# Forgetting attention's output projection: two weight splits earlier in the program, squares on ScalarE

## The chip, the cores and the metric

The kernel runs on one core of a Trainium2 chip. The metric is the device time of one execution in microseconds (us); the median of several runs counts. TensorE multiplies matrices, VectorE, ScalarE and GpSimd do elementwise work, SyncE (SP) issues most of the DMAs. In the profile's rows PE is TensorE and PEld its weight loads, DVE is VectorE, ACT is ScalarE, POOL is GpSimd; L105 is line 105 of the kernel.

## The reference

A two-layer transformer on 512 tokens of width 1024: layer 0 is forgetting attention (16 heads of 64) and a convolutional feed-forward layer, layer 1 is latent attention and another such feed-forward layer. What the change touches is the end of layer 0's attention and the beginning of its feed-forward layer:

```python
    o = lax.map(block, (jnp.arange(s_len // QBLOCK), to_blocks(q), to_blocks(cum)))
    return from_blocks(o).reshape(b, s_len, FOX_WIDTH) @ w_out
...
            x = x + fox_mixer(rmsnorm(x, fox_norm[layer]), w_fox_in[layer], b_fox_f[layer],
                              w_fox_out[layer])
...
        x = x + conv_ffn(rmsnorm(x, ffn_norm[layer]), w_ffn_in[layer], ffn_conv_w[layer],
                         ffn_conv_b[layer], w_ffn_out[layer])
```

All values are float32. So the output projection is a 512 x 1024 by 1024 x 1024 product, added to x; the root mean square of the new x over its 1024 features then scales the input of the feed-forward layer.

## The kernel before, in words

Activations lie transposed in SBUF, features on the partitions: `xT` has eight tiles of 128 features by 512 tokens. Each float32 operand of a product is split into a high part, rounded to the format that TensorE takes, and a low part, the rest; a product of a weight block with an activation block is three matmuls (`mm3`: high by high on L83, high by low on L84, low by high on L85). A step here is one such triple.

`load_w` brings in a weight. SP loads it into one of three `raw` buffers (L95), ScalarE casts it to the high part (L104), and the engine `eng`, VectorE if none is given, subtracts that from the raw weight (L105), which gives the low part. By default both go into the tags `whi` and `wlo`, of two buffers each.

The output projection has eight output tiles of 128 features, eight steps each. `wo_tile(d, pt, early)` makes a generator that does one step each time it is asked. Tiles 0 to 4 are begun inside the loop over the heads, one step at a time, to fill TensorE's holes (`FOX_FILL`); tiles 0 and 1 hold the two pairs of `whi` and `wlo`, while the weights of tiles 2 to 4 lie in buffers of the attention that are already free, loaded in halves. `fill((4,) * 7)` behind the loop does seven steps of tile 4. Each of the five has its eighth step left.

`out_proj` then takes the tiles in turn. For each it finishes the steps, adds the result in PSUM to `xT` on VectorE (L264), and splits the sum, times a gain, for the feed-forward layer: the high part on ScalarE (L188), the low part on VectorE (L189). The sum's square goes into the running sum of squares. For tiles 0 to 6 the square is a multiplication on GpSimd (L141), for tile 7 an activation on ScalarE (L139); GpSimd adds all of them up (L145). Squares and sum take buffers of the tag `r2`, of which there are four. The weights of tiles 5, 6 and 7 are loaded and split when their tile's turn comes in the program.

The feed-forward layer begins with weight blocks `in_wfi` and a step for each of the eight split tiles; the reciprocal root of the sum of squares is applied to its results, so that it is wanted only behind its first tile (L153).

Each engine executes its own instructions in order. Their order is the text's, as far as a scheduler of the framework, which lays the instructions of the whole program out before the run, doesn't let one go ahead whose operands it expects earlier.

Of the kernel before, what the change touches and what calls it, by code (L numbers as in the profile page):

```python
# [15 lines left out]
P = 128  # L16
# [3 lines left out]
KD = D // P  # L20
# [14 lines left out]
G_FOX, G_FFN, G_KVIN, G_MLA, G_KV, G_Q, G_FIN, G_N = 0, 8, 24, 32, 40, 42, 48, 56  # L35
# [10 lines left out]
def tile_kernel(ctx, tc, xT_d, gains_d, bf_d, const_d, conv_d, wv_d, wq_d, wk_d, wfo_d,  # L46
                wdq_d, wdkv_d, wuqn_d, wuqr_d, wuk_d, wuv_d, wmo_d, wfi_d, wfu_d, out_d):
    nc = tc.nc
    v, a, g, pe = nc.vector, nc.scalar, nc.gpsimd, nc.tensor
# [11 lines left out]
    def T(pool, shape, dt, tag, bufs=None):  # L61
        cnt[0] += 1
        kw = {} if bufs is None else {"bufs": bufs}
        return pool.tile(shape, dt, tag=tag, name=f"{tag}_{cnt[0]}", **kw)

    def acc():
        return T(ps, [P, 512], F32, "acc", 3)

    def att():
        return T(ps, [P, 512], F32, "att", 5)  # L70
# [4 lines left out]
    def big(k, name):  # L75
        return T(bp, [P, 8, 2, S], F32R, "big", 3)[:, :k]

    def f(ap):
        return ap.bitcast(F32)
# [7 lines left out]
    def load_w(src, shape, gain=None, eng=None, into=None, pieces=1):  # L87

        n = 1
        for s in shape[1:]:  # L90
            n *= s
        raw = T(wp, [P, 1024], F32, "raw", 3)[:, :n]
        cuts = [slice(i * n // pieces, (i + 1) * n // pieces) for i in range(pieces)]
        for c in cuts:
            nc.sync.dma_start(raw[:, c], src[:, c])  # L95
        if gain is not None:
            k, c = gain
            r3 = raw.rearrange("p (k c) -> p k c", c=n // k)
            g.tensor_tensor(out=r3, in0=r3, in1=c.unsqueeze(2).to_broadcast([P, k, n // k]), op=ALU.mult)
        if into is None:  # L100
            into = T(wp, [P, 1024], F32R, "whi", 2), T(wp, [P, 1024], F32R, "wlo", 2)
        hi, lo = (t[:, :n] for t in into)
        for c in cuts:
            a.copy(hi[:, c], raw[:, c])  # L104
            (eng or v).tensor_tensor(out=lo[:, c], in0=raw[:, c], in1=f(hi[:, c]), op=ALU.subtract)  # L105
        names = " ".join(f"d{i}" for i in range(len(shape) - 1))
        kw = {f"d{i}": shape[i + 1] for i in range(len(shape) - 1)}
        pat = f"p ({names}) -> p {names}"
        return hi.rearrange(pat, **kw), lo.rearrange(pat, **kw)
# [5 lines left out]
    def gain(base, k):  # L115
        return gains[:, base + k:base + k + 1]

    xT = cp.tile([P, KD, S], F32, name="xT")
# [63 lines left out]
    def split_x(dst, k, src, gn):  # L182

        if gn is None:
            a.copy(dst[:, k, 0, :], src)  # L185
            v.tensor_tensor(out=dst[:, k, 1, :], in0=src, in1=f(dst[:, k, 0, :]), op=ALU.subtract)
        else:
            a.activation(dst[:, k, 0, :], src, AF.Copy, scale=gn)  # L188
            v.scalar_tensor_tensor(out=dst[:, k, 1, :], in0=src, scalar=gn, in1=f(dst[:, k, 0, :]),  # L189
                                   op0=ALU.mult, op1=ALU.subtract)  # L190

    def parts(t, k, sl=slice(None)):
        return t[:, k, 0, sl], t[:, k, 1, sl]
# [52 lines left out]
    def out_tile(pt, loads, nk, src):  # L246

        k = 0
        for load, kn in loads:
            wh, wl = load()  # L250
            for kk in range(kn):
                mm3(pt, (wh[:, kk, :], wl[:, kk, :]), src(k), k == 0, k == nk - 1)
                k += 1
                yield

    def out_proj(tile_of, gbase):

        xs = big(KD, "xs")
        squares = Squares()
        for d in range(KD):  # L260
            pt, steps = tile_of(d)
            for _ in steps:
                pass
            v.tensor_tensor(out=xT[:, d, :], in0=pt, in1=xT[:, d, :], op=ALU.add)  # L264
            split_x(xs, d, xT[:, d, :], None if gbase is None else gain(gbase, d))
            squares.add(xT[:, d, :], a if d == KD - 1 else g)
        return xs, squares

    class Rstd:
# [19 lines left out]
    def ffn(layer, xs, squares, gbase):  # L289
        with tc.tile_pool(name=f"ffn{layer}", bufs=1, reuse_waits="tile") as fp:  # L290
# [42 lines left out]
            if layer < DEPTH - 1:  # L333
                return out_proj(tile_of, gbase)
# [66 lines left out]
    with tc.tile_pool(name="fx", bufs=1, reuse_waits="tile") as fp:  # L401
# [5 lines left out]
        squares = Squares()  # L407
# [107 lines left out]
        def proj_q(j):  # L515
            wh, wl = load_w(wq_d[j], [P, KD, P], eng=g)
            pt = acc()
            for k in range(KD):
                mm3(pt, (wh[:, k, :], wl[:, k, :]), parts(xn, k), k == 0, k == KD - 1)
                if k < KD - 1:  # L520
                    yield
            for e in range(2):
                t1 = T(fp, [P, S], F32R, "t1", 4)
                t2 = T(fp, [P, S], F32R, "t2", 4)
                nc.gpsimd.dma_start(t2[64:68], cum_d[0, 2 * j + e])
                src = pt[64 * e:64 * e + 64, :]
                a.activation(t1[0:64], src, AF.Copy, scale=FSCALE)
                v.scalar_tensor_tensor(out=t1[64:128], in0=src, scalar=FSCALE, in1=f(t1[0:64]),
                                       op0=ALU.mult, op1=ALU.subtract)
                a.copy(t2[0:64], f(t1[0:64]))  # L530
                qs[2 * j + e] = t1, t2
            yield

        def proj_k(j):
            wh, wl = load_w(wk_d[j], [P, KD, P], eng=g)
            pt = acc()
            for k in range(KD):
                mm3(pt, (wh[:, k, :], wl[:, k, :]), parts(xn, k), k == 0, k == KD - 1)
                if k < KD - 1:
                    yield  # L540
            for e in range(2):
                m1 = T(fp, [P, S], F32R, "m1", 2)
                m2 = T(fp, [P, S], F32R, "m2", 2)
                nc.gpsimd.dma_start(m2[64:68], cum_d[1, 2 * j + e])
                src = pt[64 * e:64 * e + 64, :]
                a.copy(m1[0:64], src)
                v.tensor_tensor(out=m2[0:64], in0=src, in1=f(m1[0:64]), op=ALU.subtract)
                a.copy(m1[64:128], f(m1[0:64]))
                ks[2 * j + e] = m1, m2
            yield  # L550

        def scores(h):
            (t1, t2), (m1, m2) = qs.pop(h), ks.pop(h)

            def passes(i, n):
                sl = slice(i * P, (i + 1) * P)
                return [(t1[:, sl], m1[:, :n]), (t2[0:68, sl], m2[0:68, :n])]

            es_h, softmax = attn_scores(fp, lambda: by_tile(passes), mask)
            softmax()  # L560
            return es_h
# [11 lines left out]
        def wo_tile(d, pt, early):  # L573
            def load(c):
                tags = (("m1", 2), ("m2", 2)) if d == 4 else (("t1", 4), ("t2", 4))
                into = [T(fp, [P, S], F32R, t, n) for t, n in tags]
                return load_w(wfo_d[d, :, c * S:(c + 1) * S], [P, KD // 2, P], eng=g, into=into)

            loads = [(lambda c=c: load(c), KD // 2) for c in (0, 1)] if early else [(lambda: load_w(wfo_d[d], [P, KD, P]), KD)]
            return pt, out_tile(pt, loads, KD, lambda k: parts(oT, k))  # L580

        def fillers():
            for j in range(1, FH // 2):
                yield from proj_q(j)
                yield from proj_k(j)
# [2 lines left out]
            for _ in u:  # L588
                pass
        es = {0: scores(0)}  # L590
        stream, ahead = fillers(), {}

        def fill(what):
            if isinstance(what, int):
                for _ in range(what):
                    next(stream)
            else:
                for d in what:
                    if d not in ahead:
                        ahead[d] = wo_tile(d, acc() if d < 2 else att(), d >= 2)  # L600
                    next(ahead[d][1])

        fill(12)
        for h in range(FH):
# [7 lines left out]
            values(h, pT, op_t)  # L612
            if h % 2:
                split_x(oT, h // 2, op_t, None)
        fill((4,) * 7)

        xs, squares = out_proj(lambda d: ahead[d] if d in ahead else wo_tile(d, acc(), False), G_FFN)

    xs, squares = ffn(0, xs, squares, None)


    with tc.tile_pool(name="ml", bufs=1, reuse_waits="tile") as mp:
# [107 lines left out]
        squares = Squares()  # L730
# [21 lines left out]
        squares = Squares()  # L752
# [16 lines left out]
        def mo_tile(d, pt):  # L769
            return pt, out_tile(pt, [(lambda c=c: load_w(wmo_d[d, :, c * D:(c + 1) * D], [P, 8, P]), 8) for c in (0, 1)],  # L770
                                MH, lambda k: parts(oTs[k // 8], k % 8))

        ahead = {}
# [16 lines left out]
        for h in range(MH):  # L790
# [23 lines left out]
            mvalues(h, pT)  # L814

        xs, squares = out_proj(lambda d: ahead[d] if d in ahead else mo_tile(d, acc()), G_FFN + KD)

    ffn(1, xs, squares, None)
# [88 lines left out]
```

## Time and profile before

| | |
|---|---|
| median of 3 runs | 1411.13 us |
| lowest and highest run | 1409.04 and 1411.53 us |
| the profiled execution, its own time | 1410.6 us |
| its span, first to last instruction | 1408.8 us |
| mean granted clock of TensorE | 0.993 |
| busy: TensorE, VectorE, ScalarE, GpSimd | 1373.6, 886.6, 648.7, 282.2 us |

The profile comes from one execution; times inside it count from the span's start. The stage of the change lies between about 234 and 270 us. The granted clock is 1.00 at 2.4 GHz and 0.50 at 1.2 GHz.

### The profile page before, as it was taken

What the parts mean: (1) busy time and instruction counts of PE and PEld (TensorE: products, weight loads), DVE (VectorE), ACT (ScalarE), POOL (GpSimd) and SP (SyncE); (2) the same over time, 40 slices, a digit from 0 to 9 for tenths busy, and PEclk for the clock granted to TensorE, in tenths of its full rate; (3) what the DMA queues carried; (4) which work ended last, traced back from release to release, by engine and by line L of the source; (5) the groups of instructions that cost most, each with busy time, mean ns of one, the idle gap of its engine ahead of it and who ended that gap; (6) DMA issues with size and microseconds to landing.
All of it is one profiled execution on the core that took longest, in us unless ns stands there. A gap on an engine that the chain in (4) does not pass through costs nothing. (4 is left out here: it accounts for less than half of the span.)

```text
span 1408.8 us, 17333 instructions
## 1 busy us (share of the span) xinstructions
PE 1373.6 (98%) x6594; PEld 1150.8 (82%) x6594; DVE 886.6 (63%) x1482; ACT 648.7 (46%) x1131; POOL 282.2 (20%) x214
## 2 busy tenths in 40 slices
PE   8999999899999999999899999999999999999997
PEld 7988888788888888888688888888888888888886
DVE  6667785677777754445866665575557777774333
ACT  4588884254444432223556555653234444442111
POOL 4343323500000001145422222212210000000222
PEclk9999999999999999999999999999999999999999
DMA  5321112232323233332121111212222322323331
GB/s 180 103 77 54 56 54 68 78 105 90 103 92 99 96 94 96 97 117 83 41 68 50 55 60 51 72 60 90 91 97 96 95 100 95 100 92 92 97 99 70
DMA packets 41252, 120.23 MB, mean 85 GB/s; under 512 B 5552, under 2 KB 9952, under 8 KB 41168
## 3 DMA queue, kind: packets, MB, share of 16 engines
q1 hardware_dynamic: 39184, 117.00, 26.0%
q0 software_dynamic: 1840, 2.09, 0.6%
q8 instruction: 51, 0.84, 0.2%
q14 instruction: 33, 0.27, 0.1%
q10 hardware_dynamic: 144, 0.03, 0.0%
HBM read 116.74 MB, written 2.36 MB: 85 GB/s over the span
## 5 line engine op out<-in xcount | busy, mean ns | idle before, releaser
L83 PE MATMUL acc<-big,whi 128*128 128x512 f32 (+1 forms) x1504 | 587.2, 391 | 2.7 <-ACT big L188 1.7
L85 PE MATMUL acc<-big,wlo 128*128 128x512 f32 (+1 forms) x1504 | 584.8, 389 | 3.5 <-DVE wlo L105 3.5
L84 PE MATMUL acc<-big,whi 128*128 128x512 f32 (+1 forms) x1504 | 584.8, 389 | 1.2 <-DVE big L189 1.2
L104 ACT CAST whi<-raw 128x1024 fp32r<-128x1024 f32 (+5 forms) x243 | 229.2, 944 | 413.8 <-PE acc L84 281.6
L85 PEld LDWEIGHTS acc<-big,wlo 128*128 128x128 f32 x1504 | 283.9, 189 | 63.4 <-DVE wlo L105 4.1
L83 PEld LDWEIGHTS acc<-big,whi 128*128 128x128 f32 x1504 | 283.6, 189 | 61.5 <-ACT big L188 3.1
L84 PEld LDWEIGHTS acc<-big,whi 128*128 128x128 f32 x1504 | 284.0, 189 | 59.1 <-DVE big L189 1.8
L105 DVE TENSOR_TENSOR wlo<-raw,whi 128x1024 fp32r<-128x1024 f32 (+3 forms) x179 | 234.6, 1310 | 141.7 <-ACT whi L104 139.1
L141 POOL TENSOR_TENSOR r<-xT 128x512 f32<-128x512 f32 x28 | 31.3, 1122 | 724.0 <-DVE xT L264 402.7
L105 POOL TENSOR_TENSOR wlo<-raw,whi 128x768 fp32r<-128x768 f32 (+3 forms) x64 | 108.0, 1687 | 251.1 <-ACT whi L104 205.5
L304 DVE SCALAR_TENSOR_TENSOR c<-u,conv,c 128x510 f32<-128x510 f32 (+1 forms) x176 | 131.2, 748 | 3.5 <-ACT c L302 0.6
L299 DVE TENSOR_TENSOR u<-acc,R 128x512 f32<-128x512 f32 x88 | 60.3, 688 | 76.3 <-PE acc L85 76.3
L214 ACT ACTIVATE e<-e,nm 128x128 f32<-128x128 f32 (+3 forms) x128 | 71.2, 557 | 41.7 <-DVE nm L208 41.7
L145 POOL TENSOR_TENSOR r<-r,r 128x512 f32<-128x512 f32 x38 | 72.1, 1898 | 28.2 <-ACT r L139 21.3
L302 ACT ACTIVATE c<-u,conv 128x512 f32<-128x512 f32 x88 | 71.3, 813 | 3.1 <-DVE u L299 2.7
L308 ACT ACTIVATE sg<-c 128x512 f32<-128x512 f32 x44 | 27.8, 632 | 78.9 <-DVE c L304 78.8
L241 DVE TENSOR_TENSOR ptl<-att,pth 128x512 fp32r<-128x512 f32 (+3 forms) x128 | 55.5, 483 | 5.9 <-ACT pth L240 5.3
L185 ACT CAST big<-sg 128x512 fp32r<-128x512 f32 x32 | 19.9, 621 | 81.7 <-DVE sg L309 81.6
L217 DVE TENSOR_SCALAR e<-e,rl 128x128 f32<-128x128 f32 (+3 forms) x128 | 55.7, 495 | 1.2
L240 ACT CAST pth<-att 128x512 fp32r<-128x512 f32 (+3 forms) x128 | 46.8, 434 | 6.1 <-PE att L237 5.5
L237 PE MATMUL att<-idf,e 128*128 128x128 f32 x320 | 43.5, 275 | 0.5
L237 PEld LDWEIGHTS att<-idf,e 128*128 128x128 f32 x320 | 36.9, 140 | 8.5 <-DVE nm L208 3.8
(183 smaller groups left out, 1473.3 us busy)
## 6 DMA issues: line engine op xcount, KB each, us to landing
raw<-in_wfi SPq DMA_DIRECT2D x88, 512.0 KB, 3.5
raw<-in_wfu SPq DMA_DIRECT2D x32, 512.0 KB, 3.5
raw<-in_wmo SPq DMA_DIRECT2D x16, 512.0 KB, 3.5
raw<-in_wfu SPq DMA_DIRECT2D x16, 384.0 KB, 3.1
raw<-in_wuqn SPq DMA_DIRECT2D x16, 384.0 KB, 2.9
raw<-in_wq SPq DMA_DIRECT2D x8, 512.0 KB, 3.5
raw<-in_wk SPq DMA_DIRECT2D x8, 512.0 KB, 3.5
raw<-in_wv SPq DMA_DIRECT2D x8, 384.0 KB, 2.9
```

The source lines that it names most:

```text
L83: pe.matmul(out, wh, xh, start=start, stop=False)
L84: pe.matmul(out, wh, xl, start=False, stop=False)
L85: pe.matmul(out, wl, xh, start=False, stop=stop)
L104: a.copy(hi[:, c], raw[:, c])
L105: (eng or v).tensor_tensor(out=lo[:, c], in0=raw[:, c], in1=f(hi[:, c]), op=ALU.subtract)
L145: (adder or g).tensor_tensor(out=self.sum, in0=self.sum, in1=sq, op=ALU.add)
L214: a.activation(es[i], es[i], AF.Exp, scale=-1.0, bias=nm[:, i:i + 1], accum_out=l[:, i:i + 1])
L217: v.tensor_scalar(out=es[i], in0=es[i], scalar1=rl[:, i:i + 1], scalar2=None, op0=ALU.mult)
L237: pe.transpose(out=pt[:, (i - j) * P:(i - j + 1) * P], in_=es[i][:, j * P:(j + 1) * P], identity=idf)
L299: v.tensor_tensor(out=u, in0=pt, in1=R, op=ALU.mult)
L302: a.activation(c, u, AF.Identity, scale=cw[:, 2:3], bias=cw[:, 3:4])
L304: v.scalar_tensor_tensor(out=c[:, s:], in0=u[:, :S - s], scalar=cw[:, 2 - s:3 - s], in1=c[:, s:], op0=ALU.mult, op1=ALU.add)
```

## The change

The last steps of tiles 0 and 1 are done first; then the weights of tile 5 (low part subtracted on GpSimd) and of tile 6 (on VectorE) are loaded and split at that place of the program, ahead of the last steps of tiles 2 to 4 and of all additions; `out_proj` picks them up when it comes to these tiles. The squares of tiles 0 to 6 are activations on ScalarE, in this projection alone. Tile 7's weight is handled as it was.

```diff
-    def out_proj(tile_of, gbase):
+    def out_proj(tile_of, gbase, eng=None):
...
-            squares.add(xT[:, d, :], a if d == KD - 1 else g)
+            squares.add(xT[:, d, :], a if d == KD - 1 else (eng or g))
...
-            loads = [(lambda c=c: load(c), KD // 2) for c in (0, 1)] if early else [(lambda: load_w(wfo_d[d], [P, KD, P]), KD)]
+            def whole():
+                return begun.pop(d) if d in begun else load_w(wfo_d[d], [P, KD, P])
+
+            loads = [(lambda c=c: load(c), KD // 2) for c in (0, 1)] if early else [(whole, KD)]
...
-        stream, ahead = fillers(), {}
+        stream, ahead, begun = fillers(), {}, {}
...
-        fill((4,) * 7)
-
-        xs, squares = out_proj(lambda d: ahead[d] if d in ahead else wo_tile(d, acc(), False), G_FFN)
+        fill((4,) * 7 + (0, 1))
+        begun[5] = load_w(wfo_d[5], [P, KD, P], eng=g)
+        begun[6] = load_w(wfo_d[6], [P, KD, P])
+        fill((2, 3, 4))
+
+        xs, squares = out_proj(lambda d: ahead[d] if d in ahead else wo_tile(d, acc(), False), G_FFN, a)
```

## Rows read from the trace of the kernel before

**Rows 1.** The page's first part: engine, busy us, share of the span, instructions.

```profile
PE 1373.6 (98%) x6594; PEld 1150.8 (82%) x6594; DVE 886.6 (63%) x1482; ACT 648.7 (46%) x1131; POOL 282.2 (20%) x214
```

**Rows 2.** TensorE's waits, 195 to 300 us: total us, times, longest.

```profile
PE acc L85 <- DVE wlo L105: 3.5, 1, 3.5
```

**Rows 3.** TensorE's timeline: start, duration (us), instruction, idle before and its releaser.

```profile
239.72 0.39 PE L83 MATMUL acc<-big,whi 128*128 128x512 f32 x1
...
243.12 0.39 PE L83 MATMUL acc<-big,whi 128*128 128x512 f32 x1
...
243.57 0.47 PE L85 MATMUL acc<-big,wlo 128*128 128x512 f32 x1
...
248.88 0.39 PE L84 MATMUL acc<-big,whi 128*128 128x512 f32 x1
250.20 0.51 PE L83 MATMUL acc<-big,whi 128*128 128x512 f32 x1 [0.93 <-ACT whi L104]
254.24 0.79 PE L85 MATMUL acc<-big,wlo 128*128 128x512 f32 x1 [3.54 <-DVE wlo L105]
...
259.37 0.39 PE L85 MATMUL acc<-big,wlo 128*128 128x512 f32 x1
...
266.87 0.39 PE L83 MATMUL acc<-big,whi 128*128 128x512 f32 x1
```

**Rows 4.** Windows: length; busy PE, PEld, DVE, ACT, POOL; clock; DMA share, GB/s.

```profile
254.20:259.10 4.90, 4.86 (x12) 3.80 (x12) 3.89 (x3) 0.72 (x1) 4.74 (x4) 0.50 0.64 206
...
240.60:258.10 17.50, 13.04 (x48) 9.95 (x47) 17.49 (x15) 6.61 (x9) 15.76 (x11) 0.84 0.25 71
```

**Rows 5.** VectorE's timeline, 240 to 270 us.

```profile
240.60 1.37 DVE L264 TENSOR_TENSOR xT<-acc,xT 128x512 f32<-128x512 f32 x2 [2.83 <-PE acc L85]
241.88 1.60 DVE L105 TENSOR_TENSOR wlo<-raw,whi 128x1024 fp32r<-128x1024 f32 x1
...
248.35 3.86 DVE L189 SCALAR_TENSOR_TENSOR big<-xT,gains,big 128x512 fp32r<-128x512 f32 x3
252.13 2.06 DVE L105 TENSOR_TENSOR wlo<-raw,whi 128x1024 fp32r<-128x1024 f32 x1
...
262.76 1.99 DVE L105 TENSOR_TENSOR wlo<-raw,whi 128x1024 fp32r<-128x1024 f32 x1 [0.21 <-ACT whi L104]
264.67 1.77 DVE L189 SCALAR_TENSOR_TENSOR big<-xT,gains,big 128x512 fp32r<-128x512 f32 x1
...
267.97 1.23 DVE L105 TENSOR_TENSOR wlo<-raw,whi 128x1024 fp32r<-128x1024 f32 x1 [0.21 <-ACT whi L104]
269.12 0.75 DVE L189 SCALAR_TENSOR_TENSOR big<-xT,gains,big 128x512 fp32r<-128x512 f32 x1
```

**Rows 6.** ScalarE's timeline, 238 to 285 us.

```profile
240.37 2.00 ACT L104 CAST whi<-raw 128x1024 fp32r<-128x1024 f32 x2 [3.32 <-PE acc L84]
...
249.12 1.03 ACT L104 CAST whi<-raw 128x1024 fp32r<-128x1024 f32 x1
...
268.46 0.62 ACT L139 ACTIVATE r<-xT 128x512 f32<-128x512 f32 x1
```

**Rows 7.** L105 on GpSimd, 60 to 240 us: ns min/median/max, first and last start.

```profile
L105 POOL TENSOR_TENSOR wlo<-raw,whi x16: 2381/2398/2660, 59.7 to 187.8; 128x1024 fp32r<-128x1024 f32 x16
```

**Rows 8.** SP's timeline, 223 to 300 us: the first row.

```profile
223.87 0.33 SPq L95 DMA_DIRECT2D raw<-in_wfo  x1
```

**Rows 9.** GpSimd's timeline, 240 to 272 us.

```profile
259.07 1.29 POOL L145 TENSOR_TENSOR r<-r,r 128x512 f32<-128x512 f32 x1
262.63 1.04 POOL L141 TENSOR_TENSOR r<-xT 128x512 f32<-128x512 f32 x1 [2.27 <-DVE xT L264]
263.75 2.15 POOL L145 TENSOR_TENSOR r<-r,r 128x512 f32<-128x512 f32 x1
```

**Rows 10.** GpSimd's groups, 240.5 to 260.4 us: busy us, mean ns of one; idle before.

```profile
L141 POOL TENSOR_TENSOR r<-xT 128x512 f32<-128x512 f32 x6 | 8.5, 1424 | 18.3 <-DVE xT L264 18.3
```

**Rows 11.** TensorE's waits, 266 to 1408 us: total us, times, longest.

```profile
PE acc L703 <- DVE Vp L707: 4.9, 7, 0.7
```

## The prediction

> **What bounds the kernel now.** The page's first part comes first: TensorE is busy for 98% of the span [rows 1]. So an edit on the other engines can only win back a stretch in which TensorE stands or runs slowly, and the thing to look for is such a stretch beside the edit. The second view is the list of what TensorE waited for from 195 to 300 us: the one that stands out is 3.5 us for the low half of a weight (L105 on VectorE) [rows 2]; a second, 0.9 us for a high half (L104 on ScalarE), lies right before it [rows 3]. The third view, TensorE's timeline, shows where they lie and what they really cost. From 239.72 to 243.12 us fifteen matmuls start in 3.40 us, 0.2267 us each; they are the eighth steps of tiles 0 to 4. At 243.12 tile 5 begins, and tiles 5, 6 and 7 are 3 x 24 = 72 matmuls, which at that pace take 16.32 us. The first matmul behind them starts at 266.87, after 23.75 us. So 7.43 us are lost here, more than the 4.4 us of the waits. Piece by piece, always less one pace of 0.23: 248.88 to 250.20 loses 1.09, 250.20 to 254.24 loses 3.81, and the twelve starts from 254.24 to 259.37 take 5.13 where 2.72 would do, 2.41 more; the remaining 0.12 is scattered.
>
> The third piece is no wait. In the windows view the granted clock is 0.50 from 254.2 to 259.1, the 1.2 GHz level [rows 4]; from 243.1 to 248.9 TensorE had run without a hole. The fall is a consequence of the two waits, and I count it with them.
>
> Why are the halves late? The matmul at 254.24 is the third of tile 6 and needs tile 6's low half. VectorE's timeline shows what that subtraction was queued behind [rows 5]: two additions at 240.60, tile 5's subtraction, two low splits of the sum (L189), three additions, three more splits, and only at 252.13 tile 6's, until 254.19. VectorE is busy for 17.49 of the 17.50 us from 240.6 to 258.1, GpSimd for 15.76 of them [rows 4]. And VectorE's rows are long: a subtraction of 1024 columns takes 1.23 us at 267.97, where nothing disturbs it, but 1.60 and 2.06 here; a split takes 0.75 at 269.12, but 3.86 for three here. The matmul at 250.20 is tile 7's first, issued ahead of tile 6's third; its high half was cast at 249.12 [rows 6], as soon as tile 5 had freed a buffer. It stands in front only because tile 6's low half was missing.
>
> **The change part by part.** *Tile 5.* Tiles 0 and 1 hold both buffer pairs until their eighth steps, so the casts can't start before 240.37, as now [rows 6]. The first ends by 240.37 + 1.03 = 241.40. GpSimd, idle then, subtracts instead of VectorE: sixteen such rows lie between 2.38 and 2.66 us, median 2.40 [rows 7]. With 0.08 to start, it ends at 241.48 + 2.40 = 243.88. TensorE wants that half at 243.57 [rows 3]; with 0.09 for signal and weight load it gets it at 243.97. Loss: **0.40 us**, between nothing (if a matmul of tile 6 fills the hole) and 0.7 (with the longest row). VectorE is rid of 1.60.
>
> *Loads.* The DMAs of tiles 5 and 6 come earlier in the program, but SP issued the last load of this matrix at 223.87 [rows 8], 16 us before a cast can use it: nothing. SP's next load needs the raw buffer that tile 5's subtraction frees, now 0.4 us later; its weight is used in the feed-forward layer's first tile more than 15 us later: nothing. On GpSimd's queue the small load of the convolution's constants goes behind the subtraction; it is wanted only after that tile: nothing.
>
> *Tile 6.* Its subtraction is now in front of the additions in the program. Its cast ends at 242.37, so two or three additions (0.69 each) still fit in front. Then it meets GpSimd. How these two get along is seen undisturbed by others at 262.63 [rows 9, 5]: GpSimd's square ends at 263.67; VectorE's subtraction, begun at 262.76, ends 1.08 after that, at 264.75; GpSimd's addition of squares, begun at 263.75, ends 1.15 after that, at 265.90; VectorE's split, begun at 264.67, ends 0.54 after that, at 266.44. They take turns. By turns tile 6's subtraction ends at 243.88 + 1.08 = 244.96; it is wanted near 249.4. Four us to spare: the 3.81 go, and with them the reason for the matmul issued out of turn (1.09) and the low clock (2.41).
>
> *Squares.* Tiles 0 to 6 move from GpSimd to ScalarE, 7 x 0.62 = 4.3 us there [rows 6]; ScalarE has idle time enough, being busy for 6.61 us of 17.5 [rows 4]. GpSimd is rid of six squares inside this window, 8.5 us of busy time [rows 10], so VectorE waits for fewer turns. Without this cover the price would be the later cast of tile 7.
>
> *What is late next.* Tile 7's low half. It is wanted at 243.97 + 48 x 0.2267 = 254.85. Count the turns: GpSimd's addition of squares 1 has its operand at about 244.8 (cast, then two splits and two squares on ScalarE, 242.3 + 4 x 0.62) and holds from 244.96 to 246.11; split 0 ends at 246.65, split 1, alone, at 247.35; three additions run to 249.4 at 0.68 a piece [rows 5]; split 2, alone, to 250.1; then in turn GpSimd 251.25, split 3 251.8, GpSimd 252.95, split 4 253.5, GpSimd 254.65 (VectorE adds tile 5 meanwhile), and tile 7's subtraction 255.73. With 0.06 for the signal it is **0.94 us** late. Ends: nothing, if an addition slips into the turn of tile 6 or the squares come later than VectorE's splits; 2.4, if split 5 and one more turn (0.54 + 1.15) come in front. I take the count's own value, as its steps come from handovers measured in this stage.
>
> The Trainium skill's page "SBUF — State Buffer", section "SBUF: two separate sides", speaks against putting a split on GpSimd: VectorE instructions with two SBUF inputs and GpSimd instructions share one port pair under an exclusive lock, and the later one blocks for the whole instruction. The handovers agree with it to about 0.2 us. By that rule the sum is the one with 0.94; by mere slowing in proportion the sum would lack it, 1403.6 us.
>
> *Sum.* 7.43 removed, 0.40 + 0.94 = 1.34 new: a gain of 6.1 us. Behind this stage the largest sum of TensorE's waits is 4.9 us, in seven pieces of at most 0.7 in the second attention [rows 11]; nothing there hangs on when this stage ends, so the gain reaches the end. The profiled execution took 1410.6 (span 1408.8 and 1.8 around it): 1404.5. The median of the runs is 0.5 higher, which would give 1405.0; I say **1404.7 us**, between the two.
>
> **The rivals.** *Tile 7 inherits the stall.* If its subtraction comes 2.4 late with tile 5's at 0.55, and the clock falls again (2.41), the new loss is 5.4, the gain 2.1: 1408.5; with half of the lateness about 1407. For it: VectorE has no gap now, and the program order leaves tile 7 last. Against it: 1.60 and most of GpSimd's 8.5 are gone, and 4.9 us of standing preceded the fall of the clock, twice this.
>
> *No turns lost.* The 0.94 doesn't arise: 1403.6. For it: additions read PSUM and kept 0.69 throughout, so a luckier order hides GpSimd's turns. Against it: the three splits at 248.35 were all stretched, by 1.6 together.
>
> *The order isn't changed as written.* The rows of before do not stand in the order of the text (the subtraction of tile 5 ran ahead of splits 0 and 1), so a scheduler arranges them. If tile 6's subtraction still comes last on VectorE, only 1.60 goes: it ends near 252.6, TensorE waits 3.5, the clock falls (2.41), tile 5 costs 0.4: gain 1.1, 1409.5. For it: that rearrangement. Against it: where two instructions are ready, the rows follow the text's order, and the text now has this one in front.
>
> *Slower.* ScalarE takes its instructions in order. A square needs one of four buffers, and the fourth square after the first can have one only when GpSimd has added square 1; tile 7's cast may be queued behind it. If GpSimd ran as late as now, with its addition of tile 5's square ending at 260.4 [rows 9], that cast would end near 262.9 where 254.4 is needed: 8.5, with 2.41 and 0.4 a loss of 11.3 against 7.43, so 1414.5. It decides once the cast ends after 261.8. Against it: by the count the first addition ends at 246.1, many us before that square.
>
> **How the numbers follow.** The forecast, new losses between 0.6 and 2.5 us, 1403.8 to 1406.2 (the upper end on the median's scale), has 0.67; no turns lost 0.08; tile 7 inherits 0.12; order unchanged 0.08; slower 0.05. A measurement of this kernel can tell 0.2%, 2.8 us, from no change, so faster means below 1408.3. The first two and most of the third are faster: 0.85; the rest of the third and the fourth 0.10; slower 0.05. The range begins at 1402.2, 1 us under the best case without any new loss, 1403.2, as the runs of before spread by 2.5, and reaches to the far end of tile 7's case, 1408.5; what is outside is the order unchanged, the slower one and a little on the lower side.
>
> **What would show it.** Tile 6's low half ends on VectorE by 246, and no TensorE wait for L105 of 3 us remains; tile 5's comes on GpSimd at 241.5 with 2.4 us, with a hole of at most 0.7 before the matmul of 243.57; the granted clock is 1.00 from 243 to 260; the first matmul of the feed-forward layer starts near 260.5 instead of 266.87; eight L139 rows on ScalarE instead of one; everything behind is early by the same amount. Wrong would be: a wait of 2 us or more at tile 7, with a low clock behind it; tile 6's subtraction behind splits 2 to 4; or a feed-forward layer that starts early and gives the time back later.

## The result, and the profile after

| | before | after |
|---|---|---|
| median of 6 runs | 1410.89 us | 1403.62 us |
| lowest and highest run | 1409.04, 1411.53 | 1400.32, 1405.92 |
| the profiled execution, its span | 1410.6, 1408.8 | 1404.52, 1402.7 |

The ratio is 0.9949, 95% interval 0.9935 to 0.9963: the change saves 7.3 us. The lines below answer to those of before.

The first part of the page of after (compare [rows 1]):

```profile
PE 1371.8 (98%) x6594; PEld 1150.1 (82%) x6594; DVE 884.5 (63%) x1481; ACT 653.5 (47%) x1138; POOL 273.7 (20%) x208
```

GpSimd has 8.5 us less, ScalarE 4.8 more. TensorE executes the same 6594 matmuls, so the gain must be standing time and clock.

TensorE's waits from 195 to 300 us in after: total us, times, longest (compare [rows 2]):

```profile
PE acc L568 <- DVE ptl L241: 0.6, 2, 0.4
PE acc L85 <- POOL wlo L105: 0.3, 1, 0.3
```

The 3.5 us for a low half from VectorE are gone; 0.3 for one from GpSimd has come.

TensorE's timeline of after (compare [rows 3]), and one window of it: length; busy PE, PEld, DVE, ACT, POOL; granted clock; DMA share and GB/s (compare [rows 4]):

```profile
241.94 0.39 PE L83 MATMUL acc<-big,whi 128*128 128x512 f32 x1
242.17 0.39 PE L84 MATMUL acc<-big,whi 128*128 128x512 f32 x1
242.85 0.50 PE L85 MATMUL acc<-big,wlo 128*128 128x512 f32 x1 [0.30 <-POOL wlo L105]
243.19 0.39 PE L83 MATMUL acc<-big,whi 128*128 128x512 f32 x1
...
253.87 0.44 PE L85 MATMUL acc<-big,wlo 128*128 128x512 f32 x1
254.15 0.40 PE L83 MATMUL acc<-big,whi 128*128 128x512 f32 x1
...
258.92 0.39 PE L83 MATMUL acc<-big,whi 128*128 128x512 f32 x1
```

```profile
241.90:258.90 17.00, 16.70 (x73) 13.37 (x73) 15.82 (x14) 9.69 (x15) 10.59 (x8) 1.00 0.32 106
```

Tile 5 starts at 241.94, the feed-forward layer at 258.92: 16.98 us, against 23.75 before [rows 3] and 16.32 at full pace. Two holes are left: at tile 5's low half (242.17 to 242.85, 0.45 more than the pace of 0.23, and 0.11 more behind it) and, barely visible, 0.05 at tile 7's (253.87 to 254.15). No matmul is issued out of turn, and the clock is 1.00 throughout, where it had been 0.50 for 4.9 us [rows 4].

VectorE's timeline of after (compare [rows 5]), then GpSimd's:

```profile
239.42 1.37 DVE L264 TENSOR_TENSOR xT<-acc,xT 128x512 f32<-128x512 f32 x2 [2.82 <-PE acc L85]
240.78 0.69 DVE L264 TENSOR_TENSOR xT<-att,xT 128x512 f32<-128x512 f32 x1
241.39 2.49 DVE L105 TENSOR_TENSOR wlo<-raw,whi 128x1024 fp32r<-128x1024 f32 x1
243.81 3.48 DVE L189 SCALAR_TENSOR_TENSOR big<-xT,gains,big 128x512 fp32r<-128x512 f32 x2
...
251.44 0.68 DVE L264 TENSOR_TENSOR xT<-acc,xT 128x512 f32<-128x512 f32 x1
252.04 1.72 DVE L105 TENSOR_TENSOR wlo<-raw,whi 128x1024 fp32r<-128x1024 f32 x1
253.68 1.78 DVE L189 SCALAR_TENSOR_TENSOR big<-xT,gains,big 128x512 fp32r<-128x512 f32 x1
```

```profile
240.38 2.42 POOL L105 TENSOR_TENSOR wlo<-raw,whi 128x1024 fp32r<-128x1024 f32 x1 [17.69 <-ACT whi L104]
...
243.57 3.17 POOL L145 TENSOR_TENSOR r<-r,r 128x512 f32<-128x512 f32 x2 [0.24 <-ACT r L139]
249.31 3.36 POOL L145 TENSOR_TENSOR r<-r,r 128x512 f32<-128x512 f32 x2 [2.57 <-ACT r L139]
```

The subtraction of 241.39 is tile 6's; it now stands third on VectorE, behind three additions, and that of 252.04, tile 7's, is right behind tile 5's addition and ahead of its split. The ends fit together: GpSimd's subtraction ends at 242.80, VectorE's 1.08 later, at 243.88, GpSimd's first addition of squares and VectorE's first split follow in turn.

In the profiled pair the stage gives 6.77 us. The spans differ by 6.1, since this execution came to tile 5 1.18 us earlier (243.12 against 241.94) and was 1.85 us slower behind the stage. That 6.1 is also the forecast gain is chance. The start of tile 5 lies between 241.94 and 244.79 in the ten kernels measured here, and the time behind the stage between 1134.0 and 1138.3; neither follows the edits, as e7, with after's order of instructions, has 244.11 and 1136.0. The medians differ by 7.3, nearer to the stage's 6.77.

### The profile page after: what moved, and what is told of

Read it like the earlier page. It is cut to its first block, busy times and chain, and to the rows that moved or that the text cites. A ratio compares the mean times of both kernels' runs of the same rounds, so it can differ in the third digit from the quotient of the medians.

```text
span 1402.7 us, 17339 instructions
## 1 busy us (share of the span) xinstructions
PE 1371.8 (98%) x6594; PEld 1150.1 (82%) x6594; DVE 884.5 (63%) x1481; ACT 653.5 (47%) x1138; POOL 273.7 (20%) x208
## 4 chain that ended last, share of the span: by engine, by line
PE 47%; ACT 2%; DVE 1%; issue 0%; POOL 0%; DVEq 0%; ACTq 0%
PE acc L84 13%; PE acc L83 13%; PE acc L85 13%; PE att L203 3%; PE acc L731 2%; ACT e L214 1%; PE att L237 1%; ACT pth L240 1%; DVE ptl L241 0%; PE acc L709 0%; PE att L83 0%; DVE r L675 0%; PE att L85 0%; DVE o L378 0%; PE att L84 0%; PE acc L711 0%
## 5 line engine op out<-in xcount | busy, mean ns | idle before, releaser
L105 DVE TENSOR_TENSOR wlo<-raw,whi 128x1024 fp32r<-128x1024 f32 (+3 forms) x178 | 234.0, 1314 | 139.8 <-ACT whi L104 137.3
L105 POOL TENSOR_TENSOR wlo<-raw,whi 128x256 fp32r<-128x256 f32 (+3 forms) x65 | 110.5, 1701 | 268.6 <-ACT whi L104 226.5
L141 POOL TENSOR_TENSOR r<-xT 128x512 f32<-128x512 f32 x21 | 21.9, 1041 | 703.5 <-DVE xT L264 382.1
```

## The experiments

All are measured with one ruler, the stage: from tile 5's first matmul to the matmuls of L153 behind the feed-forward layer's first tile, less that tile's own 24 x 0.2267 = 5.44 us. At full pace it is 16.32. The rest is the time from L153 to the end of the span. Stage and rest come from one profiled execution each, the ratios, to runs of before on the same chip, from several runs; the median of before was 1410.75 beside e1 to e4 and 1411.62 beside e5 to e8. The differences between the variants are mostly smaller than the intervals, so they are read from the stage. Three things change: the place in the text (the move), the engine of tile 5's subtraction, and the engine of the squares. Before, after, e1, e2, e3, e5, e6 and e7 are all eight combinations of them; e4 and e8 are extra questions.

| kernel | stage | rest | median, us | ratio, 95% interval |
|---|---|---|---|---|
| before | 23.75 | 1136.5 | 1410.89 | |
| after | 16.98 | 1138.3 | 1403.62 | 0.9949, 0.9935 to 0.9963 |
| e1_squares_only | 18.18 | 1138.1 | 1406.6 | 0.9968, 0.9958 to 0.9979 |
| e2_order_only | 19.05 | 1136.1 | 1406.51 | 0.9966, 0.9954 to 0.9977 |
| e3_both_vector | 18.50 | 1136.9 | 1406.07 | 0.9966, 0.9953 to 0.9979 |
| e4_swapped | 16.64 | 1136.1 | 1403.73 | 0.9947, 0.9932 to 0.9963 |
| e5_order_vector | 18.49 | 1137.3 | 1406.55 | 0.9959, 0.9945 to 0.9974 |
| e6_g5_only | 19.06 | 1136.8 | 1406.14 | 0.9958, 0.9944 to 0.9971 |
| e7_g5_squares | 16.99 | 1136.0 | 1405.55 | 0.9960, 0.9945 to 0.9974 |
| e8_late2 | 22.6 | 1134.0 | 1407.45, one run | |

**Squares alone.** Before, with its squares on ScalarE (and `out_proj` taking the engine as in the change); nothing moved in the text, all subtractions on VectorE.

```diff
-        xs, squares = out_proj(lambda d: ahead[d] if d in ahead else wo_tile(d, acc(), False), G_FFN)
+        xs, squares = out_proj(lambda d: ahead[d] if d in ahead else wo_tile(d, acc(), False), G_FFN, a)
```

> The squares of tiles 0 to 6 on ScalarE, nothing reordered: both weights are split where they were. The stage is counted from tile 5's first matmul to the feed-forward layer's first: 23.75 us before, 16.98 in the changed kernel, 16.32 without any loss. Theory (the place of tile 6's subtraction on VectorE is the cause): it still stands behind five additions, tile 5's subtraction and five splits, 3.4 + 1.23 + 3.5 us of work from 240.6 on and up to four turns of GpSimd of 1.15, so it ends 0.8 to 5 us after it is wanted; stage 18 to 22 us, a third to two thirds of the gain. Rival (GpSimd's squares in VectorE's way are the cause): stage below 17.5 us, the whole gain of about 7 us.

The stage is 18.18, at the lower end of what was expected: 5.57 of the 7.43 come back without any move of the text, but not the whole. TensorE's timeline, VectorE's, then a window behind the wait (columns as above):

```profile
252.40 0.50 PE L85 MATMUL acc<-big,wlo 128*128 128x512 f32 x1 [1.56 <-DVE wlo L105]
```

```profile
250.04 2.30 DVE L105 TENSOR_TENSOR wlo<-raw,whi 128x1024 fp32r<-128x1024 f32 x1
```

```profile
252.50:258.00 5.50, 5.50 (x25) 4.53 (x26) 4.21 (x5) 1.75 (x3) 2.51 (x2) 1.00 0.48 146
```

TensorE still waits for tile 6's low half, but stands idle for 1.56 us instead of 3.54; the clock behind it stays at 1.00 and no matmul goes out of turn. So moving GpSimd's squares takes away a large part of the stall. It does so in two ways that this run can't separate: VectorE loses fewer turns, and its order is another one, with tile 6's subtraction behind four splits where it had stood behind five [rows 5].

**Order and GpSimd's subtraction alone.** After, with its squares on GpSimd.

```diff
-        xs, squares = out_proj(lambda d: ahead[d] if d in ahead else wo_tile(d, acc(), False), G_FFN, a)
+        xs, squares = out_proj(lambda d: ahead[d] if d in ahead else wo_tile(d, acc(), False), G_FFN)
```

> Both splits ahead, tile 5's on GpSimd, but the squares stay on GpSimd. Theory (place on VectorE, with GpSimd as the cover that the squares on ScalarE buy): tile 6's wait is gone, but GpSimd does the first square before tile 5's subtraction, which is then 1.0 to 1.5 us later, and its squares take turns from tile 7's subtraction, which comes 2 to 4 us late; stage 18.5 to 21 us. Rival (the order alone is the cause): stage 17 to 17.5 us, gain 6 to 7 us.

19.05, within what was expected. TensorE's timeline, then GpSimd's:

```profile
245.14 0.50 PE L85 MATMUL acc<-big,wlo 128*128 128x512 f32 x1 [1.06 <-POOL wlo L105]
...
257.39 0.50 PE L85 MATMUL acc<-big,wlo 128*128 128x512 f32 x1 [1.03 <-DVE wlo L105]
```

```profile
241.72 1.04 POOL L141 TENSOR_TENSOR r<-xT 128x512 f32<-128x512 f32 x1 [17.51 <-DVE xT L264]
242.72 2.38 POOL L105 TENSOR_TENSOR wlo<-raw,whi 128x1024 fp32r<-128x1024 f32 x1
```

Two waits, one at tile 5, where GpSimd takes square 0 in front of the subtraction, and one at tile 7. That second one is, in a smaller form, what the prediction had feared for the whole change: with the squares still in the turns it comes, but it is 1.2 us where 2 to 4 were expected here, and the clock does not fall.

**Both subtractions on VectorE.** After, with tile 5's subtraction on VectorE.

```diff
-        begun[5] = load_w(wfo_d[5], [P, KD, P], eng=g)
+        begun[5] = load_w(wfo_d[5], [P, KD, P])
```

> As the changed kernel, but tile 5's subtraction on VectorE too. Theory (only the place in VectorE's queue matters, and GpSimd's slower subtraction costs 0.4 us at tile 5): no wait at tile 5, none at tiles 6 and 7, since GpSimd holds the ports 2.4 us less while VectorE works 1.23 us more; stage 16.3 to 16.6 us, 0.4 to 0.6 better than the changed kernel. Rival (VectorE had too much to do, so that a split had to leave it): tile 7's subtraction comes late, stage above 17.5 us.

18.50: my theory missed, and what the rival forecast came. TensorE's timeline, VectorE's, ScalarE's, and a window behind the wait:

```profile
256.81 0.50 PE L85 MATMUL acc<-big,wlo 128*128 128x512 f32 x1 [1.84 <-DVE wlo L105]
```

```profile
242.24 2.35 DVE L105 TENSOR_TENSOR wlo<-raw,whi 128x1024 fp32r<-128x1024 f32 x2
...
251.64 2.89 DVE L189 SCALAR_TENSOR_TENSOR big<-xT,gains,big 128x512 fp32r<-128x512 f32 x2
254.45 2.30 DVE L105 TENSOR_TENSOR wlo<-raw,whi 128x1024 fp32r<-128x1024 f32 x1
```

```profile
252.90 1.03 ACT L104 CAST whi<-raw 128x1024 fp32r<-128x1024 f32 x1
```

```profile
256.90:262.00 5.10, 5.10 (x23) 4.17 (x24) 2.25 (x3) 1.26 (x3) 1.52 (x1) 1.00 0.62 200
```

The first two subtractions are quick, 2.35 us for both, but tile 7's comes behind two more splits and ends at 256.75: the stall is passed on to tile 7, with the clock at 1.00 behind it. ScalarE's order has a part in this: tile 7's cast, at 252.90, now stands behind the split and the square of tile 5, and in after, at 250.33, ahead of them, so the subtraction could not have begun before 253.93. Beside the other two edits GpSimd's 2.4 us for one subtraction are worth having (16.98 against 18.50), though VectorE would do it in 1.2.

**Swapped.** Tile 5 on VectorE, tile 6 on GpSimd.

```diff
-        begun[5] = load_w(wfo_d[5], [P, KD, P], eng=g)
-        begun[6] = load_w(wfo_d[6], [P, KD, P])
+        begun[5] = load_w(wfo_d[5], [P, KD, P])
+        begun[6] = load_w(wfo_d[6], [P, KD, P], eng=g)
```

> As the changed kernel, but tile 5's subtraction on VectorE and tile 6's on GpSimd. Theory: tile 5's half is ready by 243.2 on the clock of before (cast to 241.4, then 1.23 behind two additions), tile 6's on GpSimd by 245, four us early; stage 16.3 to 16.6 us. Rival (turns on the shared ports decide): GpSimd's 2.4 us hold the splits of tiles 0 and 1 back, so that tile 7's subtraction is 0.5 to 1.5 us late; stage 16.9 to 18 us.

16.64, just above what was expected and below the rival's range: the 0.56 at tile 5 are gone, 0.29 arise at tile 7. After's stage is 0.34 longer, and the medians (1403.73 and 1403.62) don't tell them apart. VectorE's timeline, then GpSimd's:

```profile
242.90 1.22 DVE L105 TENSOR_TENSOR wlo<-raw,whi 128x1024 fp32r<-128x1024 f32 x1
244.04 2.89 DVE L189 SCALAR_TENSOR_TENSOR big<-xT,gains,big 128x512 fp32r<-128x512 f32 x1
```

```profile
243.52 2.87 POOL L105 TENSOR_TENSOR wlo<-raw,whi 128x1024 fp32r<-128x1024 f32 x1 [18.65 <-ACT whi L104]
```

One split, 0.75 us when undisturbed [rows 5], takes 2.89: it stands until GpSimd's subtraction ends at 246.39 and ends 0.54 after it, the very handover that the prediction had read from before.

**Order alone, all on VectorE.** The edit of e3 and that of e2 together.

> Both splits ahead, both subtractions on VectorE, squares on GpSimd: the move in the text alone. The instructions of VectorE and GpSimd are those of before in another order. Theory (a backlog of fixed size; the move only changes which tile meets its end): tile 7's subtraction ended 13.3 us after tile 5's first matmul before, and ends there again; tile 7 wants it 11.3 us after; tiles 5 and 6 don't wait; so one wait of 1.6 to 2.4 us at tile 7, no matmul out of turn, clock 1.00, stage 18.0 to 18.9 us (before 23.75, changed kernel 16.98). Rival (tile 7 inherits the whole stall, low clock with it): stage above 20.5 us.

18.49, inside what was expected, but not as expected: tile 7's subtraction ends 12.3 us after tile 5's first matmul, not 13.3, and the lateness is in two places. TensorE's timeline, then GpSimd's:

```profile
256.41 0.50 PE L85 MATMUL acc<-big,wlo 128*128 128x512 f32 x1 [0.76 <-DVE wlo L105]
...
267.99 0.49 PE L153 MATMUL att<-small,r 128*128 128x2 f32 x3 [0.81 <-POOL r L145]
```

```profile
264.96 2.97 POOL L145 TENSOR_TENSOR r<-r,r 128x512 f32<-128x512 f32 x2
```

0.9 at tile 7, and 0.97 at L153 (a start 1.20 after the matmul before it, less the pace), where TensorE waits for GpSimd's last additions of squares, until 267.93. With squares and additions on GpSimd the sum itself comes late. This is the plainest test of order: the instructions of both engines are those of before, and another order alone wins 5.26 us of the stage.

**Tile 5's subtraction on GpSimd alone, nothing moved.** Against before.

```diff
-            loads = [(lambda c=c: load(c), KD // 2) for c in (0, 1)] if early else [(lambda: load_w(wfo_d[d], [P, KD, P]), KD)]
+            loads = [(lambda c=c: load(c), KD // 2) for c in (0, 1)] if early else [(lambda: load_w(wfo_d[d], [P, KD, P], eng=g if d == 5 else None), KD)]
```

> One word against the kernel before: tile 5's subtraction on GpSimd, nothing moved in the text, squares on GpSimd. With VectorE free at that moment the scheduler itself puts tile 6's subtraction behind the third addition and ahead of all splits. Theory (what counts is the place on VectorE, not the place in the text): wait of 0.4 to 0.5 us at tile 5, none at tile 6, 0.8 to 1.6 at tile 7 by GpSimd's turns; stage 17.6 to 18.5 us. Rival (the move in the text is needed): stage above 20 us, as forecast for an order that stays as it was.

19.06, more than expected: GpSimd again took square 0 first (at 241.99, the subtraction at 242.99), which I had left out, and TensorE waits 1.07 at tile 5 and 1.07 at tile 7. VectorE's timeline:

```profile
242.58 0.69 DVE L264 TENSOR_TENSOR xT<-att,xT 128x512 f32<-128x512 f32 x1
243.19 3.27 DVE L105 TENSOR_TENSOR wlo<-raw,whi 128x1024 fp32r<-128x1024 f32 x1
246.38 4.67 DVE L189 SCALAR_TENSOR_TENSOR big<-xT,gains,big 128x512 fp32r<-128x512 f32 x3
```

Tile 6's subtraction stands right behind the third addition, as in after, although in the text it comes behind the additions of tiles 0 to 5. The scheduler put it there once tile 5's had left VectorE. The rival, that the move in the text is needed, falls; and e2, the same kernel with the move, has the same stage (19.05).

**The same with squares on ScalarE.** After without the move of the text.

> The changed kernel without its move in the text: tile 5's subtraction on GpSimd, squares on ScalarE. Theory: the same order on every engine as in the changed kernel where it matters, stage 16.8 to 17.2 us, gain 6.5 to 7 us of the stage. Rival (the move has a share of its own): stage above 17.5 us.

16.99, after's 16.98. TensorE's timeline, then VectorE's:

```profile
245.01 0.50 PE L85 MATMUL acc<-big,wlo 128*128 128x512 f32 x1 [0.29 <-POOL wlo L105]
```

```profile
243.56 2.49 DVE L105 TENSOR_TENSOR wlo<-raw,whi 128x1024 fp32r<-128x1024 f32 x1
```

The same hole of 0.3, the same subtraction of 2.49. Given the other two edits, the move is worth nothing in this stage. The median, 1405.55, is 1.9 higher than after's, but the intervals overlap, and before was 0.7 higher beside e7 (1411.62 against 1410.89).

**Tile 7's low half made late.** After, with tile 7's subtraction done three times over, to see whether one long wait brings the low clock.

```diff
-            (eng or v).tensor_tensor(out=lo[:, c], in0=raw[:, c], in1=f(hi[:, c]), op=ALU.subtract)
+            for _ in range(1 + again):
+                (eng or v).tensor_tensor(out=lo[:, c], in0=raw[:, c], in1=f(hi[:, c]), op=ALU.subtract)
```

> The changed kernel with tile 7's subtraction done three times on VectorE (same result), to make one wait of known length with no matmul out of turn. By the rows of the changed kernel the third ends about 3.9 us after it is wanted. Theory (the low clock was a consequence of the waits): the granted clock falls behind the wait, which costs 2 to 2.5 us more, stage 22.8 to 23.6 us. Rival (the fall had another reason, or needs more): clock 1.00, stage 20.5 to 21.2 us.

The stage is 22.6, 5.6 more than after's, from a single execution. TensorE's timeline (the lines of the kernel are one lower here, so L106 is the subtraction), and a window:

```profile
255.33 0.39 PE L84 MATMUL acc<-big,whi 128*128 128x512 f32 x1
259.58 0.80 PE L85 MATMUL acc<-big,wlo 128*128 128x512 f32 x1 [3.86 <-DVE wlo L106]
...
263.02 0.40 PE L84 MATMUL acc<-big,whi 128*128 128x512 f32 x1
```

```profile
259.50:262.70 3.20, 3.12 (x7) 2.48 (x8) 2.42 (x4) 1.24 (x2) 1.16 (x1) 0.50 0.58 169
```

A hole of 4.02 (4.25 less the pace), and behind it the granted clock is at its lower level, 0.50: the eight starts up to 263.02 take 3.44 where 1.81 would do, 1.63 more. So the low clock comes with a long wait at another tile too, and without a matmul out of turn, as the theory had it; but it cost 1.63 where 2 to 2.5 were expected, and the stage is just under its 22.8.

## Why the prediction was right

**What was lost before.** The piecewise reading, 1.09 + 3.81 + 2.41 + 0.12 = 7.43, holds. The matmul out of turn and the low clock are in none of e1 to e7, each of which shortens the wait, and e8 brings the low clock back with a wait of its own. Both went with the wait, and counting them with it was right: e1 shortens the standing at tile 6 from 3.81 to 1.71 (250.46 to 252.40, less the pace), 2.1 us, and gains 5.57.

**Tile 5.** 0.40 forecast, 0.45 measured, and 0.11 at the matmul behind. GpSimd's subtraction took 2.42 against 2.40.

**Tile 6.** Its subtraction was forecast to end by turns at 244.96 on before's clock, which is 243.78 on after's (1.18 less); it ended at 243.88. What failed is the reason for its place: "in front of the additions in the program". It stood right behind the third addition also with the text unmoved (e6, e7). Three things loosen the queue of VectorE and GpSimd, the move, a subtraction on GpSimd and the squares on ScalarE, and none of them alone removes the stall:

- any one of them takes the stage from 23.75 to between 18.2 and 19.1 (e1, e5, e6);
- the move and one other, to 19.05 (e2) or 18.50 (e3);
- a subtraction on GpSimd and the squares on ScalarE together, with the move (after, e4) or without (e7), to 16.6 to 17.0.

So the move counts only where tile 5's subtraction stays on VectorE, and only with the squares on GpSimd (before to e5, 5.26); with the squares on ScalarE it is worth nothing either (e1 18.18, e3 18.50). The load of the two engines isn't everything, as e5 wins by order alone, and the prediction's stress on the place in VectorE's queue holds that far. But the last 1.2 to 2.1 us, from the stages of e1, e2, e3, e5 and e6 to 16.98, went only when both the squares and one subtraction had left their engines. How much of that last part is load and how much the scheduler's new order stays open, since its order changed with the edits (e1, e3). Squares on ScalarE cost no wait of TensorE in after; the eight rows were busy for 4.9 us.

**Tile 7.** This is the term that was mis-sized: 0.94 forecast, 0.05 measured. The lengths of the turns held, their order did not. I had let all three additions of tiles 2 to 4 wait until the first two splits were done, although the working for tile 6 allowed for one of them in front. In after the third one runs at 240.78, while GpSimd holds its subtraction (240.38 to 242.80), in 0.69 us as if alone. From there it goes by turns, four of GpSimd's before tile 7's subtraction as counted, though the second comes before split 1 instead of later: GpSimd's second pair of additions ends at 252.67, tile 7's subtraction 1.09 later, at 253.76. By the count it would have been 255.73 - 1.18 = 254.55 on this clock. Of this difference of 0.79, the addition makes 0.69; and as tile 5 lost 0.56 instead of 0.40, the half was wanted 0.16 later. Together 0.95: nothing was left of the 0.94. The case "nothing, if an addition slips into the turn of tile 6" was named as the lower bound, and not taken. It was a favourable order that nobody had planned, and a narrow one: the half was ready at 253.76, and its matmul starts at 253.87.

The Trainium skill's page "SBUF — State Buffer", section "SBUF: two separate sides", which the prediction had set beside this, has VectorE instructions with two SBUF inputs and GpSimd's exclude each other for whole instructions. The split of 2.89 us in e4 agrees with it: it ends 0.54 after GpSimd's row. So in after the 0.94 is missing although turns are lost. The rival "no turns lost" gave the time that was measured (1403.6). By its name it is wrong, and so is slowing in proportion, for which the prediction shows no working; but the reason it gave, that additions keep 0.69 and a luckier order hides GpSimd's turns, is what happened at 240.78. With 0.08 it was given too little.

**The sum.** The stage gained 6.77 where 6.1 were forecast; the tile 7 term accounts for 0.89 of the difference, tile 5's for -0.16. The median lies 1.1 under the forecast. Nothing ties the 1.85 us that the profiled after is slower behind the stage to the edit: e7, with the same order and the same stage, has the rest 1136.0, before 1136.5 and after 1138.3, and the last section shows where they part.

**The rivals.** Tile 7 does inherit a stall, of 1 to 2 us and without a fall of the clock, but only where a part of the relief is missing (e2, e3, e5, e6). The rival of an unchanged order was badly put, as the order that counts did not hang on the text. For the slower one, by ScalarE's queue and the four buffers, nothing was seen: in after no wait of TensorE for a cast shows up in this stage. Its turning point is also summed wrongly: the 261.8 leaves out the 2.41 and the 0.4 that the same paragraph adds; with them the change would have been slower once the cast ended after 259.0.

## What to carry to other kernels

Where two engines that exclude each other feed the one that bounds, count the work of both together over the stage and look at its order. Here another order of the same work won 5.26 of 7.43 us, and either cut of the work, with the order that the scheduler then made, 4.69 to 5.57; each left waits of 1 to 2 us at one tile or another, and only the two cuts together removed all but 0.3 to 0.7 us. A wait is worth more than its length when instructions are issued out of turn and the clock falls because of it, so compare the whole stretch with full pace, and don't add up the waits alone. And before moving text, look at whether the scheduler's order follows it: here, with tile 5's subtraction on GpSimd, the same order came out with the text unmoved.

## What the runs showed of the hardware that was not expected

The clock did not fall behind every hole: behind the waits of 1.56 us (e1) and 1.84 (e3) the granted clock was 1.00. Behind 3.86 in one piece (e8), as behind 0.93 and 3.54 in two [rows 3], it was 0.50, and that cost 1.63 and 2.41 us.

The granted clock at the entry to the latent attention, far behind the change, differs from execution to execution. The windows of 50 us that begin 400 us behind L153, in before:

```profile
672.30:722.30 50.00, 44.31 (x188) 34.52 (x187) 32.06 (x61) 25.20 (x47) 20.64 (x16) 0.93 0.17 48
```

In after:

```profile
664.40:714.40 50.00, 44.48 (x178) 34.62 (x177) 32.27 (x61) 23.46 (x44) 20.61 (x15) 0.90 0.16 49
```

In e8:

```profile
671.70:721.70 50.00, 43.76 (x201) 33.92 (x199) 33.61 (x69) 26.39 (x50) 20.57 (x16) 1.00 0.18 56
```

0.93, 0.90 and 1.00, and TensorE gets through 188, 178 and 201 matmuls. In the 21 other whole windows of 50 us behind L153 it reads 1.00 in all ten kernels; only in the last 34 to 38 us, at the program's end, is it lower again, 0.87 to 0.92, with no such order among the kernels. Where it is lower at the entry the rest is longer: 1138.3 and 1138.1 us at 0.90 (after, e1), 1136.5 to 1137.3 at 0.93 (before, e3, e5, e6), 1136.0 and 1136.1 at 0.97 (e2, e4, e7), 1134.0 at 1.00 (e8). A spread of some 4 us goes with this place, with the edit or without it; what sets the clock in it was not tried.
